# One more gate/up block by seven products, a second part made by an adding transfer, and later modulation sums: a hybrid decoder layer in float32

## The chip, the cores and the metric

The kernel runs on one core of one Trainium2 chip. The metric is the device time of one execution in microseconds (us), the median of three runs. Lower is better.

## What is computed

One decoder layer on 512 tokens of width 1024, all in float32:

```python
mods = (silu(c) @ w_ada + b_ada).reshape(9, D)          # shift, scale, gate for 3 sub-layers
h = rmsnorm(x, g_pre[0]) * (1 + sc1) + sh1
x = x + 0.5 * gt1 * rmsnorm((silu(h @ Wg) * (h @ Wu)) @ w_dn1, g_post[0])    # D_FF = 2816
h = rmsnorm(x, g_pre[1]) * (1 + sc2) + sh2
x = x + gt2 * rmsnorm(token_mixer(h), g_post[1])        # GLA heads and FoX attention, merged
h = rmsnorm(x, g_pre[2]) * (1 + sc3) + sh3
x = x + 0.5 * gt3 * rmsnorm((silu(h @ Wg2) * (h @ Wu2)) @ w_dn2, g_post[2])
```

## The kernel before

**Two parts.** TensorE multiplies float32 numbers as two float32r parts: a high part `hi` (the number rounded) and a low part `lo = x - hi`. A product is hi·hi + hi·lo + lo·hi, so three matmuls. For each weight tile `split` (L153 to L158) lets ScalarE (ACT) copy 128x1024 numbers of a raw tile into `whi` (L156) and VectorE (DVE) subtract to get `wlo` (L157). There are 4 raw tiles (`NRAW`) and 5 tiles each of `whi` and `wlo` (`NW`); a split needs the slot that was used five splits before, and gets it when TensorE is done with that product. `hilo` (L198 to L200) does the same for activations.

**The feed-forward layers.** The gate and up matrices are worked on in 11 blocks of 256 columns (`ffn`). Block 0 of the first layer is worked on during the start. A plain block is 96 matmuls of 512 columns (L381). Blocks 2, 3, 4, 6, 7, 8 and 9 (`SEVEN`) go through `seven`: gate and up of one block are taken as a 2x2 matrix of halves, and 7 products of 24 matmuls with 256 columns (L430) take the place of 8. What the left sides then need is 4 sums on VectorE (L414, L415, L418, L421, in place in the raw tiles) and 7 splits; the results need 5 additions out of PSUM (`plus`, L436), two products with SiLU (L457) and 4 `hilo`. The raw tiles are fetched in the order a11, a21, a22, a12; a12 is changed by L421 and then split last, as the left side of product 6 (`l4`). `u2` is the first `plus` of a block; product 3 writes the same PSUM bank and follows it.

**Order.** All loads are issued by SyncE (SP) from one queue. A scheduler sets the order on every engine; on each the order is then fixed, and an engine waits at an instruction until its inputs are there.

**Modulation.** `ada_acc` sums eight rows of blocks of `w_ada` times SiLU(c) on VectorE (L212, L214). What is left is a sum over the 128 partitions. For shifts and scales of the second and third sub-layer (`mod_cols`, 4 calls each) `mod_reduce` (L269) does it with 4 float32 matmuls of one column, which the profile shows as 8. The first four calls for the third sub-layer run during the attention; those for the second run at the end of the gate/up blocks and in `down`. For gates (`mod_gate`, 2 calls in each `down`) the sum is split in two parts, in a `wlo` tile, and two matmuls with a matrix of ones (L295, L296) add the partitions, before the matmuls of the group in which the call stands.

**Start.** `load_x` issues 8 loads of x (256 KB each) from SP, with four small loads between the first four.

## Time and profile before

| | |
|---|---|
| median of 3 runs | 1424.99 us (1424.88 to 1426.5) |
| the profiled execution's own time | 1423.47 us |
| its span, first to last instruction | 1421.7 us |
| TensorE matmul busy | 1361.7 us (96%) |
| VectorE, ScalarE, GpSimd busy | 913.4, 595.2, 206.3 us (64%, 42%, 15%) |
| mean granted TensorE clock | 0.992 of full speed |

The profile is of one execution. Busy time is the sum over an engine's instructions, whatever they waited for. Where TensorE is busy nearly all the time, other engines matter where it waits for them, and where they let it go on with fewer matmuls.

### The profile page before, as it was taken

The page shows a single profiled execution, that of the slowest core. Times are in us where ns is not written, and L with a number is a line of the kernel's source. Part 1 is how long each engine was busy: PE and PEld are TensorE (multiplying, and loading weights), DVE is VectorE, ACT ScalarE, POOL GpSimd, SP SyncE. Part 2 cuts the span into 40 slices and gives each one's busy share as a digit, 9 for nine tenths or more (in the row PEclk, how much of TensorE's full clock was granted, in tenths as well). Part 3 has the DMA queues.
Part 4 walks back from the last instruction along what each step waited for, and adds up shares of the span by engine and source line. Part 5 has one row for each costly group of instructions (what it writes and reads, how often), then busy time and mean ns, then how long its engine had stood idle before and what let it go on. Part 6 is the DMA issues. An engine that isn't in the chain of part 4 may idle for free.

```text
span 1421.7 us, 19490 instructions
## 1 busy us (share of the span) xinstructions
PE 1361.7 (96%) x7485; PEld 1146.0 (81%) x7485; DVE 913.4 (64%) x1410; ACT 595.2 (42%) x1026; POOL 206.3 (15%) x328
## 2 busy tenths in 40 slices
PE   4899999999999999999999999999999999999998
PEld 3699899878877777777888887788878989987886
DVE  6898688675266689762645546538577877867222
ACT  6444445213254476654633334423345444333121
POOL 5300000000060644340110202100060000000001
PEclk7999999999999999999999999999999999999999
DMA  9423234588336755322332222125631332346331
GB/s 323 141 70 118 76 104 133 177 281 265 93 107 189 229 159 166 90 75 84 94 105 74 74 75 60 60 74 154 217 119 53 111 119 75 104 134 202 125 118 59
DMA packets 164089, 180.84 MB, mean 127 GB/s; under 512 B 9226, under 2 KB 128118, under 8 KB 163996
## 3 DMA queue, kind: packets, MB, share of 16 engines
q1 hardware_dynamic: 163996, 179.60, 41.1%
q8 instruction: 59, 0.97, 0.3%
q14 instruction: 34, 0.28, 0.1%
HBM read 173.25 MB, written 6.32 MB: 126 GB/s over the span
## 4 chain that ended last, share of the span: by engine, by line
PE 71%; DVE 16%; DMA 4%; ACT 4%; issue 3%; POOL 1%; SPq 0%; DVEq 0%; POOLq 0%; ACTq 0%
PE mm L193 46%; PE mm L381 11%; PE mm L430 8%; DVE wlo L157 5%; DMA raw<-in_w_gu_dram 3%; PE aux L1074 1%; DVE u L200 1%; DMA raw<-in_w_dn_dram 1%; DVE t L436 1%; ACT whi L156 1%; PE mm L896 1%; PE aux L885 1%; ACT u L869 1%; PE aux L269 1%; DVE t L214 1%
## 5 line engine op out<-in xcount | busy, mean ns | idle before, releaser
L156 ACT CAST whi<-raw 128x1024 fp32r<-128x1024 f32 x262 | 273.4, 1050 | 521.5 <-PE mm L193 272.6
L157 DVE TENSOR_TENSOR wlo<-raw,whi 128x1024 fp32r<-128x1024 f32 x260 | 322.7, 1247 | 253.5 <-ACT whi L156 238.9
L193 PE MATMUL mm<-whi,u 128*128 128x512 f32 x1216 | 391.7, 398 | 1.5 <-DVE t L354 1.5
L193 PE MATMUL mm<-u,whi 128*128 128x512 f32 x896 | 288.8, 401 | 0.8 <-DVE u L1101 0.8
L430 PE MATMUL mm<-u,whi 128*128 128x256 f32 x1568 | 279.8, 281 | 7.7 <-DVE t L436 7.6
L193 PEld LDWEIGHTS mm<-whi,u 128*128 128x128 f32 x1216 | 228.2, 188 | 54.8 <-ACT u L199 1.7
L430 PEld LDWEIGHTS mm<-u,whi 128*128 128x128 f32 x1568 | 240.2, 188 | 10.9 <-DVE t L436 10.3
L193 PE MATMUL mm<-wlo,u 128*128 128x512 f32 x608 | 240.1, 395 | 0.0
L430 PE MATMUL mm<-u,wlo 128*128 128x256 f32 x784 | 219.2, 280 | 0.0
L193 PEld LDWEIGHTS mm<-u,whi 128*128 128x128 f32 x896 | 166.4, 188 | 39.0 <-DVE u L1101 1.2
L381 PE MATMUL mm<-u,whi 128*128 128x512 f32 (+1 forms) x576 | 168.5, 379 | 11.4 <-ACT u L199 10.2
L193 PE MATMUL mm<-u,wlo 128*128 128x512 f32 x448 | 177.9, 397 | 0.0
L430 PEld LDWEIGHTS mm<-u,wlo 128*128 128x128 f32 x784 | 147.4, 188 | 0.0
L193 PEld LDWEIGHTS mm<-wlo,u 128*128 128x128 f32 x608 | 114.3, 188 | 26.8
L381 PEld LDWEIGHTS mm<-u,whi 128*128 128x128 f32 x576 | 105.5, 191 | 35.4 <-ACT u L199 13.4
L381 PE MATMUL mm<-u,wlo 128*128 128x512 f32 (+1 forms) x288 | 105.5, 376 | 0.0
L193 PEld LDWEIGHTS mm<-u,wlo 128*128 128x128 f32 x448 | 84.4, 188 | 19.5
L308 POOL TENSOR_SCALAR sm<-ss 128x1 f32<-128x1 f32 x12 | 2.3, 190 | 642.2 <-ACT jk L315 642.2
L214 DVE SCALAR_TENSOR_TENSOR t<-raw,csil,t 128x512 f32<-128x512 f32 x98 | 74.4, 759 | 3.8 <-DMA raw<-in_w_ada_dram 1.1
L381 PEld LDWEIGHTS mm<-u,wlo 128*128 128x128 f32 x288 | 55.3, 192 | 10.4
L436 DVE TENSOR_TENSOR t<-mm,t 128x512 f32<-128x512 f32 x70 | 48.0, 685 | 12.1 <-PE mm L430 11.8
L842 POOL TENSOR_SCALAR u<-t,Ft 128x128 f32<-128x128 f32 (+1 forms) x64 | 42.1, 667 | 91.3 <-DMA t<-Fd 50.1
(199 smaller groups left out, 1378.2 us busy)
## 6 DMA issues: line engine op xcount, KB each, us to landing
raw<-in_w_gu_dram SPq DMA_DIRECT2D x88, 512.0 KB, 4.0
raw<-in_w_in_dram SPq DMA_DIRECT2D x64, 512.0 KB, 3.8
raw<-in_w_dn_dram SPq DMA_DIRECT2D x44, 512.0 KB, 4.9
raw<-in_w_ada_dram SPq DMA_DIRECT2D x64, 256.0 KB, 3.6
raw<-in_w_ada_dram SPq DMA_DIRECT2D x24, 512.0 KB, 4.0
u<-in_w_ada_dram SPq DMA_DIRECT2D x32, 256.0 KB, 6.5
raw<-in_w_in_dram SPq DMA_DIRECT2D x20, 256.0 KB, 2.9
u<-in_x_dram SPq DMA_DIRECT2D x16, 256.0 KB, 4.7
```

The costliest lines, as they stand in the source:

```text
L156: nc.scalar.copy(hi, raw)
L157: (eng or nc.vector).tensor_tensor(lo, raw, hi.bitcast(F32), ALU.subtract)
L193: nc.tensor.matmul(ps, a[i], b[j], start=first and n == 0, stop=last and n == 2)
L200: (eng or nc.vector).tensor_tensor(lo, src, hi.bitcast(F32), ALU.subtract)
L214: nc.vector.scalar_tensor_tensor(a, raw[:, j, :], csil[:, k:k + 1], a, ALU.mult, ALU.add)
L269: nc.tensor.matmul(ps[:, j:j + 1], a[:, j * P:(j + 1) * P], ones[:, 0:1], start=True, stop=True)
L381: nc.tensor.matmul(p_[:, ts], w_[k][i][:, cs], hs[k][e][:, ts], start=ks[0] == 0 and n == 0, stop=ks[-1] == KD - 1 and n == 3 * len(ks) - 1)
L430: nc.tensor.matmul(ps[:, j], left[i][:, k, j * P:(j + 1) * P], right(k, e), start=first and k + j + n == 0, stop=k == 3 and n == 2, skip_g ...
L436: nc.vector.tensor_tensor(o, ps, a, ALU.add)
L842: nc.gpsimd.tensor_scalar(s_at(s, i), fb[:, 0:n], -1.0, Ft[:, i, h:h + 1], ALU.mult, ALU.add)
L869: nc.scalar.activation(s_at(S[e], i), s_at(S[e], i), AF.Exp, bias=nmx[e][:, i:i + 1], accum_out=rs[e][:, i:i + 1])
L885: nc.tensor.transpose(tp[:, off:off + P], s_at(S[e], i)[:, j * P:(j + 1) * P], ident)
```

## The change

- **Blocks.** `SEVEN` is now 2 to 9, so block 5 goes through the seven products too, in both feed-forward layers: 8 blocks in a row instead of 3, a plain one and 4.
- **Second part by a transfer.** In every such block the split of product 6 is `split_added`: ScalarE writes the high part and then the negated number into the low part's tile (as float32r, thus minus the high part), and a DMA from GpSimd's queue adds the raw tile to it. The subtraction on VectorE goes away.
- **Modulation as rows.** `mod_cols` splits its sum in two parts at once; later two matmuls of 512 columns with the matrix of ones add the partitions, and four masked sums on VectorE (`tensor_tensor_reduce` with the identity) turn the row into columns. In `down` these run one group of weights later than before.
- **Gates.** The two matmuls of `mod_gate` run after the matmuls of the next group. The two parts stand in general tiles, no longer in a `wlo` slot.
- **Start.** Three of the eight loads of x are issued from ScalarE's queue.
- `seven` is rewritten as a class with the same steps.

```diff
-SEVEN = (2, 3, 4, 6, 7, 8, 9)
+SEVEN = tuple(range(2, 10))
...
-                i = nc.sync.dma_start(xt[t][h], src[t * P:(t + 1) * P, h * 512:(h + 1) * 512])
+                i = (nc.scalar if between and h else nc.sync).dma_start(
+                    xt[t][h], src[t * P:(t + 1) * P, h * 512:(h + 1) * 512])
...
-                if between:
+                if between and not h:
                     nc.sync.dma_start(*between.pop(0))
...
+    def split_added(raw, shape):
+
+        hi = sb.tile([P] + list(shape), F32R, tag="whi", bufs=NW, name=nm("whi"))
+        lo = sb.tile([P] + list(shape), F32R, tag="wlo", bufs=NW, name=nm("wlo"))
+        nc.scalar.copy(hi, raw)
+        nc.scalar.activation(lo, raw, AF.Copy, scale=-1.0)
+        nc.gpsimd.dma_start(lo.bitcast(F32), raw, accum_op=ALU.add)
+        return hi, lo
...
     def two_parts(a):
-        pair = sb.tile([P, 2, 512], F32R, tag="wlo", bufs=NW, name=nm("pair"))
-        hilo(pair[:, 0], pair[:, 1], a)
-        return pair[:, 0], pair[:, 1]
+        pair = unit(F32R), unit(F32R)
+        hilo(*pair, a)
+        return pair
...
         a = ada_acc(src)
 
+        hi, lo = two_parts(a)
+
         def rest():
-            mod_turn(shc, scc, i, ch, mod_reduce(a))
+
+            ps = aux()
+            nc.tensor.matmul(ps, ones_r, hi, start=True, stop=False)
+            nc.tensor.matmul(ps, ones_r, lo, start=False, stop=True)
+            own, col = tmp((P, P)), small(4)
+            for j in range(4):
+                nc.vector.tensor_tensor_reduce(own, ps[:, j * P:(j + 1) * P], ident, 1.0, 0.0,
+                                               ALU.mult, ALU.add, col[:, j:j + 1])
+            mod_turn(shc, scc, i, ch, col)
         return rest
...
-        ps = aux()
         hi, lo = two_parts(a)
-        nc.tensor.matmul(ps, ones_r, hi, start=True, stop=False)
-        nc.tensor.matmul(ps, ones_r, lo, start=False, stop=True)
-        nc.vector.scalar_tensor_tensor(gs, ps, factor, gs, ALU.mult, ALU.mult)
+
+        def rest():
+            ps = aux()
+            nc.tensor.matmul(ps, ones_r, hi, start=True, stop=False)
+            nc.tensor.matmul(ps, ones_r, lo, start=False, stop=True)
+            nc.vector.scalar_tensor_tensor(gs, ps, factor, gs, ALU.mult, ALU.mult)
+        return rest
...
+            if n == 1:
+                nc.vector.tensor_tensor(a21, a21, a22, ALU.add)
+                nc.vector.tensor_tensor(a11, a21, a11, ALU.subtract)
+            elif n == 3:
+                nc.vector.tensor_tensor(a21, a22, a11, ALU.subtract)
+            part = (a11, a11, a21, a21, a12, a22, a12)[n]
+            self.left.append((split_added if n in self.added else split)(part, (4, 256)))
+            if n == 4:
+                nc.vector.tensor_tensor(a12, a12, a11, ALU.subtract)
...
+        s = Seven(*gu_blocks(w_gu, jb), hs, rs, added=(6,))
+        for n in range(s.N):
+            s.prep(n)
+        for n in range(s.N):
+            s.run(n)
+        gates, ups = s.result()
...
-                if dh == 0 and k0 in (0, 4):
-                    gate(g, k0 // 4)
-                late = extra.pop(0)() if extra and dh == 0 and k0 > 4 and k0 % 4 == 0 else None
+                if dh == 0 and k0 % 4 == 0:
+                    rest = gate(g, k0 // 4) if k0 < 8 else extra.pop(0)() if extra else None
...
-                if late:
-                    late()
+                if dh == 0 and k0 % 4 == 2 and rest:
+                    rest()
```

The order on the engines moves at three places. **VectorE, second feed-forward layer, from block 8's last sums to block 9's first.** Before (L421 changes a12; then the splits of a22 and a12; L436 is `u2`; then the next block's split of a11 and its first sum L414, which reads a21 and a22):

```order
L421 TENSOR_TENSOR raw_11165<-raw_11165,raw_11159 128x1024
L157 TENSOR_TENSOR wlo_11192<-raw_11163,whi_11191 128x1024
L436 TENSOR_TENSOR t_2087_11252<-mm_11200,t_2086_11226 128x512
L157 TENSOR_TENSOR wlo_11196<-raw_11165,whi_11195 128x1024
L157 TENSOR_TENSOR wlo_11406<-raw_11397,whi_11405 128x1024
L414 TENSOR_TENSOR raw_11399<-raw_11399,raw_11401 128x1024
L436 TENSOR_TENSOR t_2088_11302<-mm_11200,t_2086_11226 128x512
L415 TENSOR_TENSOR raw_11397<-raw_11399,raw_11397 128x1024
```

Now, at the same place (L454, L167, L483, L447 and L448 are the old L421, L157, L436, L414 and L415):

```order
L454 TENSOR_TENSOR raw_11447<-raw_11447,raw_11441 128x1024
L167 TENSOR_TENSOR wlo_11474<-raw_11445,whi_11473 128x1024
L483 TENSOR_TENSOR t_2139_11535<-mm_11483,t_2138_11509 128x512
L167 TENSOR_TENSOR wlo_11689<-raw_11680,whi_11688 128x1024
L447 TENSOR_TENSOR raw_11682<-raw_11682,raw_11684 128x1024
L483 TENSOR_TENSOR t_2140_11585<-mm_11483,t_2138_11509 128x512
L448 TENSOR_TENSOR raw_11680<-raw_11682,raw_11680 128x1024
```

The split of a12 is gone from VectorE. The split of the next a11 stands ahead of L447 in every block now, and `u2` right behind the split of a22; before, both places differed from block to block.

**ScalarE at the same place.** Now (L471 is product 0's copy, L158 the high part of a12, L159 its negation, which GpSimd's queue follows with the adding transfer; then the next block's first high part):

```order
L166 CAST whi_11473<-raw_11445 128x1024
L209 CAST u_11423<-t_2116_11434 128x256
L209 CAST u_11425<-t_2116_11434 128x256
L471 COPY t_2138_11509<-mm_11482 128x512
L158 CAST whi_11477<-raw_11447 128x1024
L159 ACTIVATE wlo_11478<-raw_11447 128x1024
L166 CAST whi_11688<-raw_11680 128x1024
```

One pass of 128x1024 has come in between the high parts of a12 and of the next a11.

**TensorE, second gate of the last `down`.** Before:

```order
L193 MATMUL mm_11780<-wlo_11873,u_10053 128x512
L193 MATMUL mm_11780<-whi_11872,u_10054 128x512
L295 MATMUL aux_11898<-pair_11899,ones 128x512
L193 MATMUL mm_11777<-whi_11931,u_10289 128x512
L193 MATMUL mm_11777<-wlo_11932,u_10289 128x512
```

Now:

```order
L203 MATMUL mm_12064<-wlo_12214,u_10469 128x512
L203 MATMUL mm_12064<-whi_12213,u_10470 128x512
L317 MATMUL aux_12241<-u_12183,ones 128x512
L318 MATMUL aux_12241<-u_12184,ones 128x512
L203 MATMUL mm_12061<-whi_12247,u_10706 128x512
```

The gate's two matmuls stand two groups of 24 matmuls further down.

## Rows read from the trace of the kernel before

**Rows 1.** The page: busy time by engine, and the chain that ended last by engine.

```profile
PE 1361.7 (96%) x7485; PEld 1146.0 (81%) x7485; DVE 913.4 (64%) x1410; ACT 595.2 (42%) x1026; POOL 206.3 (15%) x328
...
PE 71%; DVE 16%; DMA 4%; ACT 4%; issue 3%; POOL 1%; SPq 0%; DVEq 0%; POOLq 0%; ACTq 0%
```

**Rows 2.** Windows: blocks 2-4, 5, 6-9 of both layers; busy us (instructions) by engine.

```profile
88.32:150.35 62.03, 60.26 (x506) 59.65 (x505) 52.41 (x63) 29.25 (x41) 0.00 (x0) 1.00 0.41 128
150.35:172.68 22.33, 22.33 (x98) 17.92 (x96) 12.17 (x15) 7.27 (x11) 0.00 (x0) 1.00 0.09 26
172.68:255.53 82.85, 80.46 (x674) 79.57 (x673) 69.57 (x82) 39.35 (x54) 0.00 (x0) 1.00 0.39 121
1099.24:1160.20 60.96, 60.12 (x506) 59.66 (x505) 51.47 (x61) 29.52 (x41) 0.00 (x0) 1.00 0.42 130
1160.20:1182.53 22.33, 22.33 (x97) 17.92 (x96) 12.16 (x15) 7.26 (x11) 0.00 (x0) 1.00 0.09 26
1182.53:1266.06 83.53, 80.81 (x674) 79.96 (x673) 69.63 (x82) 39.48 (x55) 0.00 (x0) 1.00 0.39 120
```

**Rows 3.** Timeline of VectorE, blocks 8 and 9, second layer: start, us, instruction, [idle before].

```profile
1214.35 1.22 DVE L414 TENSOR_TENSOR raw<-raw,raw 128x1024 f32<-128x1024 f32 x1 [3.18 <-DMA raw<-in_w_gu_dram]
...
1230.84 1.22 DVE L157 TENSOR_TENSOR wlo<-raw,whi 128x1024 fp32r<-128x1024 f32 x1
1231.97 0.68 DVE L436 TENSOR_TENSOR t<-mm,t 128x512 f32<-128x512 f32 x1
1232.58 2.35 DVE L157 TENSOR_TENSOR wlo<-raw,whi 128x1024 fp32r<-128x1024 f32 x2
1236.82 1.23 DVE L414 TENSOR_TENSOR raw<-raw,raw 128x1024 f32<-128x1024 f32 x1 [1.90 <-DMA raw<-in_w_gu_dram]
...
1251.87 2.35 DVE L157 TENSOR_TENSOR wlo<-raw,whi 128x1024 fp32r<-128x1024 f32 x2
```

**Rows 4.** Timeline of TensorE, same block: product 3's first matmuls; product 6's first low part.

```profile
1232.71 0.51 PE L430 MATMUL mm<-u,whi 128*128 128x256 f32 x2 [1.00 <-DVE t L436]
...
1241.90 0.28 PE L430 MATMUL mm<-u,wlo 128*128 128x256 f32 x1
```

**Rows 5.** Timeline of ScalarE, same block: the high part of a12.

```profile
1231.01 1.05 ACT L156 CAST whi<-raw 128x1024 fp32r<-128x1024 f32 x1 [1.74 <-DVE raw L421]
```

**Rows 6.** DMA issues of the whole run: count, KB each, median us from issue to landing.

```profile
raw<-in_w_gu_dram SPq DMA_DIRECT2D x88, 512.0 KB, 4.0
u<-in_w_ada_dram SPq DMA_DIRECT2D x32, 256.0 KB, 6.5
```

**Rows 7.** Timeline of TensorE in the first `down`: a modulation sum between weight matmuls.

```profile
308.16 0.39 PE L193 MATMUL mm<-whi,u 128*128 128x512 f32 x1
308.39 0.95 PE L269 MATMUL aux<-ones,t 128*128 128x1 f32 x8
309.20 0.48 PE L193 MATMUL mm<-whi,u 128*128 128x512 f32 x1
```

**Rows 8.** Groups of VectorE, shapes apart: count, busy us, mean ns of one, idle before.

```profile
L214 DVE SCALAR_TENSOR_TENSOR t<-raw,csil,t 128x512 f32<-128x512 f32 x98 | 74.4, 759 | 3.8 <-DMA raw<-in_w_ada_dram 1.1
...
L244 DVE SCALAR_TENSOR_TENSOR t<-u,csil,t 128x512 f32<-128x512 f32 x10 | 11.5, 1146 | 0.4
...
L860 DVE CUSTOM_DVE_ANT_0 u<-mm,u 128x128 f32<-128x128 f32 x16 | 4.5, 289 | 3.8 <-POOL u L844 3.2 <-PE mm L857 0.4
...
L200 DVE TENSOR_TENSOR pair<-t,pair 128x512 fp32r<-128x512 f32 x6 | 4.1, 689 | 3.3 <-ACT pair L199 3.3
```

**Rows 9.** Windows in the attention; columns as in rows 2.

```profile
500.00:520.00 20.00, 19.60 (x105) 14.33 (x103) 19.31 (x48) 14.91 (x36) 7.63 (x15) 1.00 0.43 122
540.00:560.00 20.00, 19.89 (x114) 15.72 (x114) 19.37 (x50) 12.81 (x31) 6.18 (x12) 1.00 0.56 149
```

**Rows 10.** Timeline of TensorE in the last `down`: the two gates.

```profile
1295.50 0.50 PE L295 MATMUL aux<-pair,ones 128*128 128x512 f32 x1 [0.88 <-ACT pair L199]
...
1308.37 0.49 PE L295 MATMUL aux<-pair,ones 128*128 128x512 f32 x1 [1.41 <-ACT pair L199]
```

**Rows 11.** Timeline of VectorE before the second of them: the next weights' low part.

```profile
1305.37 1.23 DVE L157 TENSOR_TENSOR wlo<-raw,whi 128x1024 fp32r<-128x1024 f32 x1 [0.84 <-ACT whi L156]
```

**Rows 12.** The chain in order of time, start of the program: start, us, what.

```profile
3.68 0.32 SPq L131
4.05 5.31 DMA u<-in_x_dram
```

More of the change, by code (lines that the diff above doesn't have):

```diff
@@ L400, in right_sides, with __init__, prep, run @@
         return [lambda k, e, s=s: s[k // 2][e][:, k % 2] for s in sums]
[L402 to L426 removed]
+    class Seven:
+        N = 7
+        def __init__(self, wa, wb, hs, rs, turned=False, added=()):
+            self.w, self.turned, self.added = (wa, wb), turned, added
+            b11, b21, b22 = [lambda k, e, k0=k0, ts=ts: hs[k0 + k][e][:, ts] for k0, ts in
+                             ((0, slice(0, 256)), (4, slice(0, 256)), (4, slice(256, 512)))]
+            t1, t2, t3, t4 = rs
+            self.right, self.left = (b11, t2, t1, t3, b21, t4, b22), []
+        def prep(self, n):
+            wa, wb = self.w
+            if n == 0:
+                wa.fetch(0, 4)
+                wb.fetch()
+                wa.fetch()
+                self.a = [wa.raw[0], wa.raw[4], wb.raw[0], wb.raw[4]]
+            a11, a12, a21, a22 = self.a
+            if n == 1:
[7 more added lines that the diff above has]
+                nc.vector.tensor_tensor(a12, a12, a11, ALU.subtract)
+        def run(self, n):
+            if n == 0:
+                self.x, self.y, self.z = [acc((P, 2, 256)) for _ in range(3)]
+            ps, first = (self.x, self.y, self.z, self.y, self.x, self.y, self.z)[n], n < 3
+            left, right = self.left[n], self.right[n]
@@ L427, in product @@
             for k in range(4):
                 for j in range(2):
-                    for n, (i, e) in enumerate(PARTS):
-                        nc.tensor.matmul(ps[:, j], left[i][:, k, j * P:(j + 1) * P], right(k, e),
-                                         start=first and k + j + n == 0, stop=k == 3 and n == 2,
-                                         skip_group_check=True)
-        def plus(ps, a, out=None):
+                    js = slice(j * P, (j + 1) * P)
+                    for m, (i, e) in enumerate(PARTS):
+                        w_, h_ = left[i][:, k], right(k, e)
+                        nc.tensor.matmul(ps[:, j], *((h_[:, js], w_) if self.turned else (w_[:, js], h_)),
+                                         start=first and k + j + m == 0, stop=k == 3 and m == 2,
+                                         skip_group_check=True)
@@ L435, in plus @@
+            if n == 0:
+                self.p1 = tmp((P, 2, 256))
+                nc.scalar.copy(self.p1, ps)
+            elif n == 1:
+                self.u2 = self.plus(ps, self.p1)
+            elif n == 3:
+                self.u3 = self.plus(ps, self.p1)
+                self.plus(self.z, self.u3, self.u3)
+            elif n == 6:
+                self.plus(self.y, self.p1, self.p1)
+                self.plus(ps, self.u2, self.u2)
+        def plus(self, ps, a, out=None):
             o = tmp((P, 2, 256)) if out is None else out
```

46 lines of the change are left out of this document (6 added, 40 removed).

## The prediction

> **What bounds the kernel now.** I read the page first: TensorE is busy 96% of the span, and the chain that ended last is TensorE for 71% and VectorE for 16% [rows 1]. So time is saved either by giving TensorE fewer columns or by taking away what it waits for. Then the windows over the blocks that the change touches. There the reader is to see three things [rows 2]. A plain block takes 22.33 us, with TensorE busy throughout. A block by seven products keeps TensorE busy for about 20.04 us (60.12 / 3). And the runs of such blocks take longer than that: 62.03 and 82.85 us in the first layer, 60.96 and 83.53 in the second, so TensorE waits 1.77, 2.39, 0.84 and 2.72 us in them, and the runs of four lose most. The eight blocks take 62.03 + 22.33 + 82.85 = 167.21 us in the first layer and 166.82 in the second.
>
> Next, what TensorE waits for. Product 3 of block 8 starts after a wait of 1.00 us for `u2` on VectorE [rows 4], and VectorE runs `u2` only at 1231.97, behind the split of a22 that began at 1230.84 [rows 3]. So VectorE's queue sets the pace at the end of a run. VectorE in turn has a cycle of its own, with the loads: L414 of block 8 starts at 1214.35 and that of block 9 at 1236.82, 22.47 us later. It consists of the work from L414 to the end of the split of a22 (at 1230.84 + 1.22 = 1232.06, so 17.71 us), which frees the raw tile, and of 4.76 us until the next a22 is there. In these 4.76 us VectorE has `u2` and two splits to do and then sits idle for 1.90 us.
>
> **Seven products eight times.** The change takes the split of a12 off VectorE: 1.22 us in each of 16 blocks. But at both places in rows 3 that split stands behind the split of a22, inside the wait for the load, which has idle time left (1.90 us, 3.18 in the cycle before). So its removal alone shortens nothing; only the idle time grows. What shortens the cycle is the place of the split of a11, which now always stands ahead of L447. Block 9 had this order already: from its L414 at 1236.82 to the end of its split of a22 (the first of the pair that begins at 1251.87, so about 1253.0) it took 16.2 us [rows 3]. With 4.76 us for the load that makes a cycle of 20.95 us.
>
> The adding transfer shares the DMA engines with the load of a22. No row of before shows such a transfer. Below, it costs nothing there, since the next load of a12, which now waits for it, used to stand in the same place. Above, it delays a22 by half of an ordinary transfer's 4.0 us [rows 6], 2.0. I take 0.2, near the lower end, since the load of a12 goes out of the way: cycle 21.15.
>
> The runs start with a lead, so the first blocks go at TensorE's pace. First layer: three blocks at 60.26 plus half of the old wait, 0.9, then five cycles of 21.15: 166.9, 0.3 less than before. Second layer, where the first three lost less and more lead is left: 60.12 + 0.2, two blocks at about 20.1 and 20.9, three cycles: 164.8, 2.0 less. Together **-2.3**. What 0.1 us more or less in the cycle does: 14 cycles follow on a first block, so 1.4 us.
>
> The adding transfer itself has to be ready for product 6. The high part of a12 ran from 1231.01 to 1232.06 [rows 5]; the second pass on ScalarE takes the same 1.05, so GpSimd can issue at 1233.1. Product 6 first reads its low part at 1241.90 [rows 4]. So 8.8 us are there for issue and transfer. Ordinary loads of the same size land after 4.0 us, and the slowest loads listed, in the burst at the start, after 6.5 [rows 6]. An adding transfer reads two operands and writes one; bounds are 4.0 and, three times that, 12.0. I take 6.5, so it is hidden. GpSimd's queue has nothing else there (0.00 us busy in all six windows [rows 2]). ScalarE pays 1.05 us per block and is busy for under half of these windows [rows 2]. SyncE's queue stands longer at the load of a12, but the load behind it, the next block's a11, waits for that block's last sum anyway.
>
> The Trainium skill has a rule against this part: its page "SBUF — State Buffer", section "Summary: rules for kernel authors", advises against hiding a transfer from GpSimd's queue under VectorE's work, since its descriptors cannot be written while VectorE holds the shared port. By that rule it would start late, in VectorE's idle time. No row of before has such a transfer. Rows do show the two engines in each other's way: VectorE's scaled sum took 1146 ns while GpSimd worked at the start, and 759 ns elsewhere [rows 8]. For the forecast I leave the 6.5 us; a late start is the first rival. On the other side, the page of the Trainium skill "DMA: Bandwidth & Descriptors", section "Anatomy of one DMA", fits 2.0 us plus bytes at 436 GB/s, an estimate of 3.2 us for 512 KB, by which the sum would stay as it is.
>
> **Modulation as rows.** One sum takes TensorE from 308.16 to 309.20, where two weight matmuls stand 0.23 us apart, so 0.81 us net; two matmuls of 512 columns take 2 x 0.23 = 0.47 [rows 7]. That is 0.34 us in each of 8 calls: -2.7. VectorE pays for it: 0.69 for the low part and four masked sums of 0.29 (the attention's reduction of the same shape), 1.85 us per call [rows 8]. In the attention VectorE is busy 19.31 and 19.37 of 20 us where TensorE is at 19.60 and 19.89 [rows 9]; there the cover is thin. Bounds for the four calls there: nothing, and 4 x 1.85 = 7.4 us. I take 1.4, nearer the lower end, since TensorE is not idle for more than 0.4 in those 20 us. Together **-1.3**.
>
> **Gates.** In the last `down` TensorE stops at both gates, for 0.88 and 1.41 us [rows 10], while the next weights' low part is ready at 1305.37 + 1.23 = 1306.60 [rows 11]. With the gates moved two groups down it can go on at 1306.6 in place of 1308.37: **-1.8**. Below: if the next weights are late too, nothing.
>
> **Start.** Three issues leave SyncE's queue; one takes 0.37 us there (from 3.68 to 4.05), and the chain runs over the loads of x for 5.31 us behind them [rows 12]. Between 0 and 3 x 0.37 = 1.1, as the loads share the same engines: **-0.6**.
>
> Sum: -2.3 - 1.3 - 1.8 - 0.6 = -6.0 us. The profiled execution took 1423.47 us, so 1417.5. The median of the runs is 1.5 above that execution, so **1419.0 us**, 0.4% less than 1424.99. Differences under 0.2% (2.85 us) cannot be told from none here.
>
> **Rivals.**
> 1. *The adding transfer comes late* (slower). Mechanism: it lands behind product 6's first low part, TensorE waits at that place in all 16 blocks. It decides from 8.8 us after ScalarE's second pass; each further us costs up to 16. At 10 us: 1.2 x 16 = 19, so 1438. For it: three streams in place of two, and rows 8. Against it: 4.0 and 6.5 [rows 6].
> 2. *The adding transfer slows the load of a22* by 0.7 us in place of 0.2. The cycle is then 21.65, 14 x 0.5 = 7.0 us more: 1426. For it: both begin within about 2 us of one another. Against it: the load of a12 no longer does.
> 3. *The attention pays for the masked sums* at 6 us in place of 1.4: 1423.6. For it, rows 9.
> 4. *VectorE was the bound by its sum of work, not by the cycle.* Then the split's removal lets TensorE go at its pace: 16 x 20.04 = 320.6 against 334.03, so -13.4 in place of -2.3: 1408. Against it: the idle 1.90 and 3.18 us ahead of L414 [rows 3].
>
> **Chances.** Forecast 0.55, rival 1 0.13, rival 2 0.17, rival 3 0.08, rival 4 0.07. Faster: most of the forecast (0.52), rival 4 and a little of rival 2: 0.61. Same: 0.03 of the forecast, half of rival 2 and most of rival 3: 0.17. Slower: 0.22. The range 1411 to 1431 takes in the forecast with its bounds (gates and start at nothing above, a cycle without the 0.2 and attention without the 1.4 below), rivals 2 and 3, and leaves out rivals 1 and 4.
>
> **What would show it.** Right: from one L447 to the next about 21 us in the later blocks, with over 2.5 us of idle time ahead of it that a load ends; product 6 without a wait; no wait at the gates; modulation sums of two matmuls that cost 0.47; eight blocks in 167 and 165 us. Wrong: TensorE waits for GpSimd's queue in product 6 (rival 1); the load of a22 takes over 5.3 us (rival 2); TensorE waits more in the attention (rival 3); blocks at 20.0 throughout (rival 4).

## The result, and the profile after

The changed kernel took **1461.34 us** (median of 4 runs, 1455.62 to 1461.75), the kernel before 1425.64 beside it (median of 4): ratio 1.0245, 95% interval 1.023 to 1.0261. It is 36 us slower; the forecast was 1419.0 with a range to 1431. The execution in the profile below took 1455.62 us for a span of 1453.9.

The page of the changed kernel, busy time by engine and the chain that ended last, answers to [rows 1]:

```profile
PE 1368.6 (94%) x7581; PEld 1152.6 (79%) x7581; DVE 928.7 (64%) x1494; ACT 620.2 (43%) x1062; POOL 221.2 (15%) x344
...
PE 63%; DVE 17%; DMA 10%; issue 4%; ACT 4%; POOL 2%; SPq 0%; DVEq 0%; ACTq 0%; POOLq 0%
```

No engine has much more to do than before. But in the chain the share of transfers has gone from 4% to 10%, and that of TensorE from 71% to 63%: the kernel now waits for loads.

Where the time went is read by taking the same matmul in both traces: the n-th weight matmul of `mm3`, of which both traces have 3288, and, in the columns at 406.70 and 1061.90, the same transposition behind the first `down` and behind `w_out`. How much later it starts than before (us):

| run | first `down` begins (278.66 before) | first `down` done (406.70) | attention done (652.40) | `w_out` done (1061.90) | in the last `down` (1296.31) | last matmul (1415.10) |
|---|---|---|---|---|---|---|
| changed | +2.73 | +9.98 | +31.44 | +31.51 | +32.50 | +32.10 |

So 2.7 us are lost by the end of the first layer's blocks, **7.3 in the first `down`, 21.4 between there and the end of the attention**, 2.4 in the second layer's blocks, and 1.8 comes back in the last `down`. (At the first matmul of the last `down`, 1288.38 before, it is +33.88; the column at 1296.31 stands behind the first gate, where 1.4 has come back already.) The two large losses lie where the modulation sums are made, not where the blocks are.

The profiled execution is the fastest of the four, 5.7 us under their median, so the pieces add up to 32.1 us and not to 36.

The windows over the eight blocks of each layer, with [rows 2] to compare (busy us of each engine, then the granted clock and the share of DMA):

```profile
87.64:258.59 170.95, 162.18 (x1346) 159.83 (x1345) 135.80 (x165) 85.23 (x118) 6.95 (x8) 1.00 0.46 129
1130.92:1299.95 169.03, 162.05 (x1346) 159.59 (x1345) 134.88 (x163) 85.67 (x118) 6.92 (x8) 1.00 0.47 130
```

Before it was 167.21 and 166.82 us; forecast were 166.9 and 164.8.

What happens in the first `down` is seen on VectorE's timeline, ahead of the first masked sum (start, us, instruction, idle time before it and what ended it). The kernel before, where L488 multiplies the first half of block 10 and L212 begins the next sum over `w_ada`:

```profile
272.50 0.69 DVE L488 TENSOR_TENSOR t<-t,mm 128x512 f32<-128x512 f32 x1 [7.70 <-PE mm L381]
...
274.60 0.49 DVE L212 TENSOR_SCALAR t<-raw,csil 128x512 f32<-128x512 f32 x1
```

and the changed one (L281 is the masked sum, L222 begins the next sum):

```profile
267.83 0.68 DVE L210 TENSOR_TENSOR u<-t,u 128x512 fp32r<-128x512 f32 x1
281.58 0.29 DVE L281 CUSTOM_DVE_ANT_0 t<-aux,ident 128x128 f32<-128x128 f32 x1 [13.07 <-PE aux L278]
...
285.17 0.48 DVE L222 TENSOR_SCALAR t<-raw,csil 128x512 f32<-128x512 f32 x1
```

VectorE stands for 13.07 us in front of the masked sum, which needs the row that TensorE makes only after block 10 (L278). Behind it in VectorE's queue, at 285.17, stands the next sum over `w_ada` (L222, then L224). Before, VectorE stood here too, for 7.70 us, but only for the first half of block 10, and the next sum began 4.1 us ahead of the first `down` (at 278.66); now it begins 3.8 us behind its start (281.38). The four raw tiles are full, and until VectorE has read them no load finds a free tile. The same stretch in the view of the transfers, 250 to 350 us in 40 slices of 2.5 us (busy tenths of the DMA engines, then GB/s):

```profile
DMA  9779886990000006889888889898505779837789
GB/s 242 225 229 304 302 236 219 350 340 24 0 0 0 0 2 219 247 308 373 294 276 284 268 286 277 294 324 240 196 13 148 236 244 325 302 93 248 229 285 339
```

and of the kernel before:

```profile
DMA  4845789400279889779879969989889977995899
GB/s 132 269 113 137 215 279 345 189 7 0 28 245 297 293 320 284 202 239 358 266 225 269 347 212 289 292 303 344 239 259 265 326 234 240 275 315 189 211 323 406
```

Before, the stream stops for two to three slices, now for six: 15 us without a load, from about 272 to 287 us, and TensorE runs out of weights:

```profile
291.19 1.65 PE L203 MATMUL mm<-whi,u 128*128 128x512 f32 x3 [4.05 <-ACT whi L166]
```

The stops cost more than their length. Windows of the first `down`, and from there to the end of the attention, before and changed; columns as in [rows 2]:

```profile
278.66:406.70 128.04, 127.78 (x562) 102.79 (x562) 69.53 (x96) 35.52 (x51) 5.74 (x16) 1.00 0.64 203
406.70:652.40 245.70, 236.10 (x1184) 183.58 (x1183) 175.65 (x401) 141.17 (x308) 100.29 (x176) 1.00 0.50 144
281.38:416.70 135.32, 129.70 (x544) 102.77 (x543) 78.06 (x137) 37.93 (x55) 6.23 (x16) 0.97 0.59 193
416.70:683.84 267.14, 243.78 (x1160) 184.82 (x1159) 184.73 (x437) 144.62 (x312) 100.27 (x176) 0.97 0.46 133
```

Of the 28.7 us that the two stretches lose, TensorE sits idle for 19.1; the other 9.6 are its own busy time, with fewer matmuls. The granted clock falls to half (1.2 instead of 2.4 GHz) around the stops: from 289.8 to 296.6 us, at the stop above,

```profile
289.80:296.60 6.80, 5.41 (x13) 4.15 (x14) 5.36 (x7) 2.61 (x3) 0.00 (x0) 0.50 0.90 299
```

and in the attention for 3.4, 10.2 and 3.4 us, from 463.9, 504.8 and 627.7 us on. Before, the mean granted clock from 44 to 1419 us is 1.00.

From 255 to 680 us VectorE waits for these rows seven times:

```profile
DVE t L281 <- PE aux L278: 33.1, 7, 13.1
```

(total, times, longest). Before, the same wait (L276 for L269) was a single one of 0.4 us in that stretch.

### The profile page after: what moved, and what is told of

It reads as the page before. It is cut to its first block, busy times and chain, and to the rows that moved or that the text cites. A ratio compares the mean times of both kernels' runs of the same rounds, so it can differ in the third digit from the quotient of the medians.

```text
span 1453.9 us, 19874 instructions
## 1 busy us (share of the span) xinstructions
PE 1368.6 (94%) x7581; PEld 1152.6 (79%) x7581; DVE 928.7 (64%) x1494; ACT 620.2 (43%) x1062; POOL 221.2 (15%) x344
## 4 chain that ended last, share of the span: by engine, by line
PE 63%; DVE 17%; DMA 10%; issue 4%; ACT 4%; POOL 2%; SPq 0%; DVEq 0%; ACTq 0%; POOLq 0%
PE mm L203 43%; PE mm L404 8%; PE mm L466 7%; DMA raw<-in_w_gu_dram 5%; DVE wlo L167 4%; ACT whi L166 2%; DMA raw<-in_w_in_dram 1%; PE aux L1118 1%; DVE t L483 1%; DMA u<-in_w_ada_dram 1%; DVE t L224 1%; DVE u L210 1%; DVE raw L447 1%; DVE u L917 1%; DMA raw<-in_w_ada_dram 1%
## 5 line engine op out<-in xcount | busy, mean ns | idle before, releaser
L166 ACT CAST whi<-raw 128x1024 fp32r<-128x1024 f32 x252 | 263.4, 1048 | 520.1 <-PE mm L203 258.5
L167 DVE TENSOR_TENSOR wlo<-raw,whi 128x1024 fp32r<-128x1024 f32 x250 | 311.2, 1247 | 253.0 <-ACT whi L166 250.9
L203 PE MATMUL mm<-whi,u 128*128 128x512 f32 x1216 | 394.1, 399 | 7.1 <-ACT whi L166 5.6
L466 PE MATMUL mm<-u,whi 128*128 128x256 f32 x1792 | 321.2, 282 | 15.7 <-DVE t L483 15.5
L203 PE MATMUL mm<-u,whi 128*128 128x512 f32 x896 | 290.0, 403 | 6.5 <-DVE sm L904 5.7
L466 PEld LDWEIGHTS mm<-u,whi 128*128 128x128 f32 x1792 | 274.5, 188 | 20.7 <-DVE t L483 15.3
L203 PEld LDWEIGHTS mm<-whi,u 128*128 128x128 f32 x1216 | 229.6, 189 | 62.8 <-ACT whi L166 6.9
L466 PE MATMUL mm<-u,wlo 128*128 128x256 f32 x896 | 251.2, 280 | 0.0
L203 PE MATMUL mm<-wlo,u 128*128 128x512 f32 x608 | 243.3, 400 | 0.7 <-DVE wlo L167 0.7
L203 PEld LDWEIGHTS mm<-u,whi 128*128 128x128 f32 x896 | 168.2, 191 | 46.1 <-DVE sm L904 6.2
L203 PE MATMUL mm<-u,wlo 128*128 128x512 f32 x448 | 179.2, 400 | 0.0
L466 PEld LDWEIGHTS mm<-u,wlo 128*128 128x128 f32 x896 | 168.8, 188 | 0.0
L404 PE MATMUL mm<-u,whi 128*128 128x512 f32 (+1 forms) x448 | 129.3, 377 | 9.7 <-ACT u L209 8.2
L203 PEld LDWEIGHTS mm<-wlo,u 128*128 128x128 f32 x608 | 115.1, 189 | 28.4 <-DVE wlo L167 2.1
L404 PEld LDWEIGHTS mm<-u,whi 128*128 128x128 f32 x448 | 82.5, 195 | 27.8 <-ACT u L209 13.0
L203 PEld LDWEIGHTS mm<-u,wlo 128*128 128x128 f32 x448 | 85.4, 191 | 20.2
L224 DVE SCALAR_TENSOR_TENSOR t<-raw,csil,t 128x512 f32<-128x512 f32 x98 | 76.1, 777 | 8.5 <-DMA raw<-in_w_ada_dram 6.4
L404 PE MATMUL mm<-u,wlo 128*128 128x512 f32 (+1 forms) x224 | 80.6, 372 | 0.0
L160 POOL DMA_DIRECT2D wlo<-raw x16 | 13.9, 867 | 376.2 <-ACT wlo L159 376.2
L209 ACT CAST u<-t 128x256 fp32r<-128x256 f32 (+1 forms) x106 | 46.4, 455 | 29.7 <-DVE t L533 15.4
L483 DVE TENSOR_TENSOR t<-mm,t 128x512 f32<-128x512 f32 x80 | 54.8, 685 | 4.0 <-PE mm L466 3.9
```

What stands on the lines that cost most here:

```text
L166: nc.scalar.copy(hi, raw)
L167: (eng or nc.vector).tensor_tensor(lo, raw, hi.bitcast(F32), ALU.subtract)
L203: nc.tensor.matmul(ps, a[i], b[j], start=first and n == 0, stop=last and n == 2)
L209: nc.scalar.copy(hi, src)
L224: nc.vector.scalar_tensor_tensor(a, raw[:, j, :], csil[:, k:k + 1], a, ALU.mult, ALU.add)
L404: nc.tensor.matmul(p_[:, ts], w_[k][i][:, cs], hs[k][e][:, ts], start=ks[0] == 0 and n == 0, stop=ks[-1] == KD - 1 and n == 3 * len(ks) - 1)
```

## The theories

**Theory A.** Each masked sum has a throw-away output, `own`, from the ring of four `tmp` buffers that the sums over `w_ada` come from too. With it in the ring, the order that is fixed when the kernel is built puts the masked sums ahead of the next modulation's sums; VectorE works in order, waits for TensorE, and the raw tiles stay full. **Rival B:** the masked sums cost their own time. **Rival C:** the adding transfers do it. For the sevens: **D**, the adding transfer slows the load of a22 beside it (rival 2 of the prediction); **E**, eight sevens without a plain block between them run at their buffer loop anyway; **G**, the extra pass on ScalarE.

The built order of VectorE shows what A speaks of. Before, in the attention (L212 and L214 are the next modulation's sum, L276 uses the columns of the one before):

```
L212 TENSOR_SCALAR t_772_4426<-raw_4427,csil 128x512
L214 SCALAR_TENSOR_TENSOR t_772_4426<-raw_4427,csil,t_772_4426 128x512
...
L214 SCALAR_TENSOR_TENSOR t_772_4426<-raw_4442,csil,t_772_4426 128x512 x2
L157 TENSOR_TENSOR wlo_4303<-raw_4300,whi_4302 128x1024
L276 SCALAR_TENSOR_TENSOR scc_3821<-aux_4272,cols 128x2
```

Now the next sum (L222) stands behind the masked sums (L281) of the one before:

```
L281 ISA t_764_4421,sm_4422<-aux_4418,ident 128x128
L281 ISA sm_4422 128x1
...
L297 TENSOR_TENSOR shc_3962<-sm_4422,cols 128x2
L222 TENSOR_SCALAR t_802_4576<-raw_4577,csil 128x512
```

## Experiments on the modulation sums

**1. The throw-away output into the sum's own buffer.**

```diff
-            own, col = tmp((P, P)), small(4)
+            col = small(4)
...
-                nc.vector.tensor_tensor_reduce(own, ps[:, j * P:(j + 1) * P], ident, 1.0, 0.0,
+                nc.vector.tensor_tensor_reduce(a[:, j * P:(j + 1) * P], ps[:, j * P:(j + 1) * P], ident, 1.0, 0.0,
```

> The changed kernel, but the throw-away output of the masked sums is written over the sum's own buffer and takes no buffer of the ring of four. Theory A (that buffer puts the masked sums ahead of the next modulation's sums in VectorE's queue, VectorE waits for TensorE, the raw buffers stay full and the weight stream stops): VectorE's waits for the row matmuls fall from 33 us to under 6 us, the stretch from the first down product to the end of attention loses some 28 us, time 1425 to 1432. Rival B (the masked sums cost time as such, whatever stands behind them): 1450 to 1461. Rival C (the adding transfers do the damage there): unchanged, 1458 to 1461.

Measured: 1437.9 us, ratio 1.0099 (1.0079 to 1.012). The wait for the rows is gone, from 33.1 us to

```profile
DVE t L281 <- PE aux L278: 1.9, 2, 1.0
```

and the first `down` costs nothing any more (+1.37 at its beginning, +1.11 at its end). The masked sums are all still there, so B cannot hold for `down`, nor C. But the attention still loses 8.0 us (+1.11 to +9.13), more than A said: the time is 6 us above its range.

**2. Columns again, all else as changed.**

```diff
-        hi, lo = two_parts(a)
-
         def rest():
...
+            mod_turn(shc, scc, i, ch, mod_reduce(a))
         return rest
```

> The changed kernel with the later modulation sums as columns again, all else as changed. Theories A and B: the 28 us of the first down product and attention come back, what is left is the sevens' loss of 3 to 6 us less gates and start: 1425 to 1431. Rival C (adding transfers): still 1450 to 1461.

Measured: 1433.01 us, ratio 1.0062 (1.0047 to 1.0077). First `down` +3.29 to +3.53, attention to +5.16: 1.6 us. So 27 to 28 us go with the rows, and C is out. What is left is somewhat more than foreseen.

**3. Rows alone, in the kernel before.** The edit is that of `mod_cols` and `two_parts` in the change.

> The kernel before with only the modulation rows and masked sums. Theories A and B: nearly the whole loss of the change, 1448 to 1458. Rival C (it needs the adding transfers): 1422 to 1427. The sum on record gave this part -1.3 us, 1423.6.

Measured: 1454.94 us, ratio 1.0214 (1.0199 to 1.0229). The part that the forecast had at -1.3 us costs 31 by itself: +0.44, +8.27, +30.95 at the first three places of the table.

**9. The ring buffer alone.** The kernel before, with its column sums; the four columns pass through one more buffer of the ring.

```diff
-            mod_turn(shc, scc, i, ch, mod_reduce(a))
+            ps = mod_reduce(a)
+            own = tmp((P, P))
+            nc.vector.tensor_copy(own[:, 0:4], ps)
+            mod_turn(shc, scc, i, ch, own)
```

> The kernel before with its column sums, and one buffer more of the ring of four per modulation sum: the four columns of the result are copied into it before they are used (one VectorE instruction of about 0.1 us, eight times). Theory A (the place in the ring orders VectorE's queue, not the masked sums' own time): the next modulation's sums stand behind the wait for TensorE, 1440 to 1455. Rival B (the masked sums' own time): eight tiny copies cost under 1 us, 1424 to 1427.

Measured: 1451.42 us, ratio 1.0177 (1.0159 to 1.0195): eight copies of 0.16 us cost **26 us**. VectorE's timeline at the first of them:

```profile
264.77 1.22 DVE L157 TENSOR_TENSOR wlo<-raw,whi 128x1024 fp32r<-128x1024 f32 x1
279.99 0.16 DVE L265 COPY t<-aux 128x4 f32<-128x4 f32 x1 [14.00 <-PE aux L272]
...
280.46 0.49 DVE L212 TENSOR_SCALAR t<-raw,csil 128x512 f32<-128x512 f32 x1
```

It is the picture of the changed kernel without a masked sum in it, the half clock included (a mean of 0.69 from 288 to 299 us). Theory A is shown: the place in the queue costs the time. In the first `down` the reason for that place is in the built programs: in the changed kernel and in run 9 the next sum gets the very buffer (the same address) that the extra tile has just had, so it cannot begin before that tile is read; in the kernel before and in run 1 it gets the one of block 10's first half, which is free sooner. In the attention it is another buffer. Which rule at build time makes this order out of one buffer more was not tried; that it does so is seen in the orders of the changed kernel and of runs 3 and 9, and that it doesn't without that buffer, in those of the kernel before and of run 1.

**8. Rows in the first `down` only**, with the output of run 1; columns in the attention.

```diff
+        if i == 2:
+            return lambda: mod_turn(shc, scc, i, ch, mod_reduce(a))
         hi, lo = two_parts(a)
```

> The changed kernel with the throw-away output in the sum's own buffer, rows only in the first down product and columns in attention. Theory F (what the run with the throw-away output moved still lost in attention, 8.0 us against 1.6 us with columns, is VectorE's extra work and its wait of 10 us for ScalarE's first parts of the sums): attention loses about 1.6 us, time 1430 to 1434. Rival (the 8 us there come from something that the down product leaves behind): 1436 to 1439.

Measured: 1431.12 us, ratio 1.0044 (1.0029 to 1.006). The attention loses 2.6 us (+1.40 to +4.01) where run 1 lost 8.0. So the rest of run 1 came from the rows in the attention. There VectorE does more (155.6 us busy in the 204 us from 446 to 650, against 148.4 in the 198 us from 448 to 646 in run 2), and it stands longer before the low parts, for ScalarE. Waits of VectorE from 440 us on to the end of the attention, run 1:

```profile
DVE u L210 <- ACT u L209: 10.0, 4, 4.4
```

In run 2 that wait is 3.5 us in two. Which of the two costs the time was not separated.

## Experiments on the blocks by seven

For these a cycle is cut in two: from one block's first addition (L447 in the changed kernel) to the end of the split of a22 on VectorE, which frees the raw tile of a22; and from there to the next block's first addition, which needs the next a22. Taken are all cycles under 26 us, from each kernel's profile; the means in us (time and ratio are of all executions of the run):

| kernel | cycles | whole | to a22's release | release to next addition | time, us | ratio to before |
|---|---|---|---|---|---|---|
| before | 6 | 21.84 | 17.15 | 4.69 | | |
| changed | 12 | 21.81 | 16.58 | 5.23 | 1461.34 | 1.0245 |
| 4: eight sevens, adding transfer | 12 | 22.17 | 16.61 | 5.57 | 1436.37 | 1.008 |
| 5: eight sevens, no transfer | 12 | 21.20 | 16.42 | 4.78 | 1425.61 | 1.0004 |
| 6: transfer, block 5 plain | 6 | 22.50 | 17.15 | 5.35 | 1427.66 | 1.002 |
| 10: half the bytes by transfer | 12 | 22.48 | 16.61 | 5.87 | 1442.01 | 1.0112 |
| 13: plain write beside | 12 | 22.75 | 16.52 | 6.23 | 1445.06 | 1.0151 |
| 14: extra ScalarE pass only | 12 | 21.41 | 16.59 | 4.83 | 1426.28 | 1.0002 |
| 15: transfer in two | 12 | 22.15 | 16.61 | 5.54 | 1434.89 | 1.0073 |

**4. Sevens and adding transfer alone, in the kernel before.** The edit is `SEVEN`, `split_added` and the class `Seven` of the change.

> The kernel before with block 5 by seven products and the last second part of every seven by the adding transfer, nothing else. If the two gate/up stretches lose here what they lose in the changed kernel (3.7 and 2.2 us): 1428 to 1433. The sum on record gave -2.3 us, 1422.7. By rival C 1450 or more.

Measured: 1436.37 us, ratio 1.008 (1.0061 to 1.0099), more than the two stretches of the changed kernel had said. The loss lies in the blocks: +6.92 at the end of the first layer's, and 6.2 more (from +9.67 to +15.91) by the beginning of the last `down`. The profiled execution, 1440.6 us, is the slowest of the four, so these pieces are somewhat too large.

**5. Block 5 by seven, without the transfer.**

```diff
-SEVEN = (2, 3, 4, 6, 7, 8, 9)
+SEVEN = tuple(range(2, 10))
```

> The kernel before with block 5 by seven products as well, no adding transfer. Theory D (the adding transfer makes the a22 load longer, and that load sits in the loop that sets a seven's period): with no such transfer each layer gains the plain block's 22.33 less 20.3 to 21.2 us, 1421 to 1424. Rival E (without a plain block between them the eight sevens run at their buffer loop, 21.5 us or more each, whether a transfer adds or not): 1428 to 1436, as with the adding transfer (1436.4).

Measured: 1425.61 us, ratio 1.0004 (0.9992 to 1.0017): no difference. It falls between the two expectations. E as stated is out, since eight sevens in a row run at 21.20 us a cycle. Of the gain that D gave, the profile shows -1.3 us at the end of the first layer's blocks; in the second layer 0.9 us are lost by the beginning of the last `down` (from -1.00 to -0.12). The ten executions of run 5 lie between 1421.35 and 1428.4 us, so pieces of about 1 us from one profile are no more than a hint. The adding transfer costs 11.8 us (+12.3 against +0.5, each to the kernel before beside it); 12 cycles, each 0.97 longer, make 11.6.

The reason is in the second half of the cycle. VectorE's timeline of run 4, the split of a22 and the next block's first addition (L433):

```profile
1202.17 1.22 DVE L166 TENSOR_TENSOR wlo<-raw,whi 128x1024 fp32r<-128x1024 f32 x1
...
1208.89 1.23 DVE L433 TENSOR_TENSOR raw<-raw,raw 128x1024 f32<-128x1024 f32 x1 [2.33 <-DMA raw<-in_w_gu_dram]
```

and of run 5 (the first of the pair is the split of a22, the second that of a12; L414 is the addition):

```profile
1168.23 2.35 DVE L157 TENSOR_TENSOR wlo<-raw,whi 128x1024 fp32r<-128x1024 f32 x2
...
1174.13 1.23 DVE L414 TENSOR_TENSOR raw<-raw,raw 128x1024 f32<-128x1024 f32 x1 [1.81 <-DMA raw<-in_w_gu_dram]
```

From the split's end to the addition it is 1208.89 - 1203.39 = 5.50 us in run 4 and 1174.13 - 1169.45 = 4.68 in run 5. Both times a load ends the wait. The split that the transfer replaces stands behind a22's release, so taking it away shortens nothing, and the load gets longer. What stands beside it has changed: SyncE issues the load of a22 0.06 us after the release in both runs, but the next load of a12 1.6 us after it in run 5 and 8.1 in run 4 (means), where that tile is free only when the transfer has landed. The transfer, issued 0.6 to 1.3 us after the release, takes the place beside the load of a22 that the load of a12 had.

**6. The adding transfer with block 5 plain.** The edit of run 4 with `SEVEN` as before.

> The kernel before with block 5 plain as it was and the adding transfer in the seven others. Theory D: 0.6 to 1 us lost per seven that follows a seven, 1430 to 1436. Rival E: no loss, 1422 to 1426.

Measured: 1427.66 us, ratio 1.002 (1.0009 to 1.0032), under the range of D though the cycles are longer by 0.66 (22.50 against 21.84). In this profile the first layer loses 2.85 us by the end of its blocks, the second 0.3 (from +3.84 to +4.10). That a plain block in the middle gives VectorE and the loads a lead of which the delay is paid would explain it; it was not tested. So the transfer and the eighth seven cost 2.6 and 0.5 us alone and 12.3 together.

**10. Half the bytes by the transfer.**

```diff
-        nc.scalar.activation(lo, raw, AF.Copy, scale=-1.0)
-        nc.gpsimd.dma_start(lo.bitcast(F32), raw, accum_op=ALU.add)
+        nc.scalar.activation(lo[:, 2:4], raw[:, 2:4], AF.Copy, scale=-1.0)
+        nc.gpsimd.dma_start(lo[:, 2:4].bitcast(F32), raw[:, 2:4], accum_op=ALU.add)
+        nc.vector.tensor_tensor(lo[:, 0:2], raw[:, 0:2], hi[:, 0:2].bitcast(F32), ALU.subtract)
```

> The run with eight sevens and the adding transfer, but the transfer takes half of the second part (256 KB) and VectorE the other half. Theory D (the transfer lengthens the a22 load that runs beside it): the stretch from the release of a22's buffer to the next block's first addition lies between 4.8 us (no transfer) and 5.6 us (512 KB), the time between 1425.6 and 1436.4: 1428 to 1433. Rival (a fixed price per transfer: its issue and ScalarE's extra pass): 1435 to 1438.

Measured: 1442.01 us, ratio 1.0112 (1.0098 to 1.0126): not between, but above. Half the bytes take nearly as long. The view of the transfers from 90 to 250 us, run 4 (KB each, median us to landing; then the queue's packets, MB and share):

```profile
q0 software_dynamic: 1008, 3.67, 11.6%
...
wlo<-raw POOLq DMA_DIRECT2D x7, 512.0 KB, 7.1
```

and run 10:

```profile
q0 software_dynamic: 1008, 1.84, 6.3%
...
wlo<-raw POOLq DMA_DIRECT2D x7, 256.0 KB, 6.3
```

The packets are as many (144 for each), the transfer is beside the load nearly as long. So the price does not go with the bytes, though the forecast had it so. One thing more differs: ScalarE's second pass is half as long, and the transfer is issued 0.55 us after a22's release (mean) where run 4 has 0.97. Whether the earlier start makes the dearer cycle was not tested.

**13. A plain write beside**, VectorE makes the low part.

```diff
-        nc.scalar.activation(lo, raw, AF.Copy, scale=-1.0)
-        nc.gpsimd.dma_start(lo.bitcast(F32), raw, accum_op=ALU.add)
+        nc.vector.tensor_tensor(lo, raw, hi.bitcast(F32), ALU.subtract)
+        away = dr.tile([P] + list(shape), F32, tag="away", bufs=2, name=nm("away"))
+        nc.gpsimd.dma_start(away, hi.bitcast(F32))
```

> Eight sevens, VectorE makes every second part (no adding transfer), and a plain, not adding transfer of 512 KB beside: the first part of the last piece is written out to DRAM from GpSimd's queue, after ScalarE has made it. Nothing waits for it. Theory D1 (any transfer beside the a22 load lengthens it): release of a22's buffer to next first addition 5.2 to 5.6 us, 1431 to 1437. Theory D2 (only the adding kind does, or its waits): 4.8 us as without, 1424 to 1427.

Measured: 1445.06 us, ratio 1.0151 (1.0119 to 1.0183), above the range. A write that nothing waits for costs 19 us: the second half of the cycle is 6.23 us. So a transfer need not be an adding one to lengthen the load of a22. How dear adding itself is, the run does not say: without it the load of a12 is back beside that of a22 (1.6 us after the release) and the write is a third stream, issued 0.1 us after the release on the mean.

**14. The extra pass on ScalarE without a transfer.**

```diff
-        nc.gpsimd.dma_start(lo.bitcast(F32), raw, accum_op=ALU.add)
+        nc.vector.tensor_tensor(lo, raw, hi.bitcast(F32), ALU.subtract)
```

> Eight sevens, no adding transfer, but ScalarE's second pass over the last piece is kept (VectorE then overwrites it). Theory G (a fixed price from ScalarE's extra pass): 1430 to 1437. Theories D1 and D2: 1424 to 1428.

Measured: 1426.28 us, ratio 1.0002 (0.999 to 1.0014). G is out: the pass is hidden.

**15. The transfer in two.**

```diff
-        nc.gpsimd.dma_start(lo.bitcast(F32), raw, accum_op=ALU.add)
+        for k in (0, 2):
+            nc.gpsimd.dma_start(lo[:, k:k + 2].bitcast(F32), raw[:, k:k + 2], accum_op=ALU.add)
```

> Eight sevens, the adding transfer as two of 256 KB each: the same bytes, twice the packets (288 for 144 per seven). If packets set what the a22 load loses (half the bytes in as many packets lost as much): the stretch grows from 5.6 to 6 us or more, 1442 to 1450. If the number of transfers or their bytes do not matter beside: 1435 to 1438.

Measured: 1434.89 us, ratio 1.0073 (1.0049 to 1.0096), as run 4. Twice the packets cost nothing more. So neither bytes nor packets scale the price, within 256 to 512 KB; what in the transfer does stays open. In all four runs the price is higher where the transfer is issued sooner (1.00, 0.97, 0.55 and 0.11 us after the release in runs 15, 4, 10 and 13), but the changed kernel, at 0.99, pays less than run 4, and no run moves the start alone.

## Experiments on gates and start, and the best version

**7. Gates later and x by two queues, nothing else.** The changed kernel with `SEVEN` of before, `added=()` and the columns of run 2.

> The changed kernel without its two other parts: sevens as before (block 5 plain, no adding), modulation sums as columns; what is left is the gate matmuls later and x by two queues. The sum on record gave -1.8 and -0.6 us: 1421 to 1423. Rival: the last modulation's later place costs what the gates give, 1424 to 1426.

Measured: 1423.12 us, ratio 0.9981 (0.9969 to 0.9994), -2.0 us where -2.4 was forecast. In its profile TensorE is 1.3 us ahead when block 2 begins, 0.4 behind when the last `down` begins (first matmul +0.36) and 2.0 ahead at the end.

**11 and 12. What gains, together.** Run 7 with the rows of run 8 in the first `down`; in run 11 also eight sevens without a transfer in the first layer alone, in run 12 not.

```diff
-        s = Seven(*gu_blocks(w_gu, jb), hs, rs, added=(6,))
+        s = Seven(*gu_blocks(w_gu, jb), hs, rs, added=())
...
-        by_seven=SEVEN, keep=(2, lambda tp, k: h3[tp, k // 2]), source=xe)
+        by_seven=(2, 3, 4, 6, 7, 8, 9), keep=(2, lambda tp, k: h3[tp, k // 2]), source=xe)
```

> What the runs so far say gains, together: gate matmuls later, x by two queues (-2.0 us together), rows in the first down product alone with the throw-away output in the sum's own buffer (-1.9), block 5 by seven without an adding transfer in the first layer alone (-1.3). Sum 1425.1 - 5.2 = 1420: 1418 to 1423. If the parts don't add up: 1423 to 1426.

Measured: 1420.32 us, ratio 0.9964 (0.9951 to 0.9976).

> The same with block 5 plain in both layers: 1.3 us more than with eight sevens in the first layer, 1420 to 1424; if block 5 by seven gave nothing there, the same time.

Measured: 1424.39 us, ratio 0.9994 (0.9984 to 1.0003): the rows gave nothing here, and the eighth seven 4.1 us, three times what run 5 had shown.

**16 and 17. The best again, beside the same without rows.** Run 17 is the kernel of run 11; run 16 has columns in the first `down`.

> Gates later, x by two queues, eight sevens without an adding transfer in the first layer alone, and modulation sums as columns everywhere. If the rows in the first down product give nothing (the run with block 5 plain and the rows took 1424.4, the one without the rows 1423.1): as fast as the best so far, 1419 to 1422. If they give 1.9 us, as the two earlier runs with the adding transfer had it: 1422 to 1424.

Measured: 1424.61 us, ratio 0.999 (0.998 to 1.0).

> The kernel of the best run once more, beside it on one chip: 1419 to 1422 if that time was no accident of its chip; 1423 or more if it was.

Measured: 1419.96 us, ratio 0.9963 (0.995 to 0.9976). So the version of runs 11 and 17 beats the kernel before by 0.37% and the changed one by 41 us, twice. The rows in the first `down` and the eighth seven in the first layer give that only together (4.6 us between runs 16 and 17, 4.1 between 12 and 11). In the first layer's blocks and `down` run 17 is 4.56 us ahead of before, run 16 2.96; why the one needs the other was not found.

## Why the prediction was wrong

**Modulation rows: the step that failed.** Forecast -1.3 us, measured +31 alone (run 3). The matmuls' own cost on TensorE was right: a row sum costs 0.46 us where 0.47 was forecast [rows 7]. Changed kernel, TensorE's timeline in the first `down`:

```profile
322.49 0.40 PE L203 MATMUL mm<-whi,u 128*128 128x512 f32 x1
322.73 0.40 PE L277 MATMUL aux<-u,ones 128*128 128x512 f32 x1
322.96 0.39 PE L278 MATMUL aux<-u,ones 128*128 128x512 f32 x1
323.19 0.40 PE L203 MATMUL mm<-whi,u 128*128 128x512 f32 x1
```

The mistake is in "VectorE pays for it: 0.69 for the low part and four masked sums of 0.29", with "Bounds for the four calls there: nothing, and 4 x 1.85 = 7.4 us". That prices the new instructions by their busy time and takes the upper bound from it too. An instruction that waits for TensorE costs what stands behind it: here the sums that free the raw tiles, behind them the loads, behind them TensorE. The first of these waits was 13.07 us alone, and after the stops TensorE ran at half its granted clock on top. Rival 3 named the attention as the place and VectorE as the engine, but priced it by the same busy time, and nothing was said of the first `down`, where 7.3 us went. What is left when the order is mended, 8.0 us in the attention against 1.6 with columns, is 6.4: there the bound of 7.4 did hold, and the value taken (1.4, "nearer the lower end, since TensorE is not idle") was wrong.

**Sevens: the second step.** Forecast -2.3, measured +12.3 alone (run 4). Two of its pieces held. The split taken off VectorE shortens nothing: run 5 has it, runs 4 and 15 don't, and the first half of the cycle is 16.42 us in the one and 16.61 in the others. And rival 1 was rightly set low: the transfer landed 6.4 us after its issue in the median, where 6.5 had been taken; page of the changed kernel:

```profile
wlo<-raw POOLq DMA_DIRECT2D x16, 512.0 KB, 6.4
```

and it was there 1.4 to 4.2 us before product 6 read it, in all 16 blocks. It was issued 0.3 us after ScalarE's second pass ended, never later. So the late start under VectorE's work, which the prediction drew from the Trainium skill's page "SBUF — State Buffer", section "Summary: rules for kernel authors", is not in this trace, though VectorE is busy for 79% of the first layer's window (135.80 of 170.95 us). That rule speaks of a VectorE in its 2x or 4x mode, a condition that the prediction left out; the trace does not tell the mode of an instruction. The estimate of 3.2 us by the Trainium skill's page "DMA: Bandwidth & Descriptors", section "Anatomy of one DMA", is half of what was measured.

What was mis-sized is the contention: "I take 0.2, near the lower end, since the load of a12 goes out of the way". Measured 0.45 in the changed kernel (5.23 against 4.78) and 0.79 in run 4; rival 2 had 0.7. The load of a12 did go out of the way, but the adding transfer took its place: it is issued 0.6 to 1.5 us after the release of a22 (1224.93 against 1223.69 in one block of the second layer) and takes 6.4, so it lies beside nearly the whole load of a22. Rival 2's mechanism is what happened, and its price per cycle was near.

The number to start from was wrong as well. Without the 0.2 in each of its 14 cycles the forecast stood at -5.1 (its sum gives only eight cycles the full 21.15, so the 14 do not fit it); run 5, without any contention, measured +0.5. Its cycle is 21.20 us where 20.95 had been worked out from [rows 3], and from block 2's first matmul to block 10's it takes 165.8 us in the first layer and 167.4 in the second (before 167.0 and 166.7), where 166.9 and 164.8 had been forecast with the 0.2. So the lead that the second layer was to have is not there; why was not found.

**Gates and start: right in the sum, partly by luck.** Forecast -1.8 and -0.6; run 7 gives -2.0 for both. The wait at the gates [rows 10] is gone. But the sum priced the second gate alone and put the first at nothing without a reason; in run 7 the first gives 1.1 us (from +0.36 to -0.76) and the second 1.2 (to -2.00). And the start gave 1.3 us by block 2, twice the forecast, of which nothing is left at the last `down`. In the changed kernel, behind the later place TensorE waits 0.75 us for weights (L203, at 1340.70), which the lower bound had foreseen.

The parts do not add up: +31, +12.3 and -2.0 make 41, and the change costs 36. That the sevens' delay is partly covered where VectorE and the loads are late already would explain it; it was not tested.

## What to carry to other kernels

An instruction that waits is priced by what stands behind it on its engine, in the built order, and by who waits for that; its own microseconds were the smallest part here (0.16 us a copy in run 9). Before a scratch output takes a buffer from a small ring, look where the ring's other users end up in the queue; write it over something that is dead. And a transfer put beside a load that sets the pace cost that load 0.45 to 1.45 us a cycle here, and what it freed elsewhere gained nothing: first ask which half of the loop the freed work stands in.

## What was not expected of the hardware

A transfer's price to a load beside it did not go with its bytes: 256 KB cost the a22 load 1.1 us (5.87 against 4.78), 512 KB 0.8 (5.57), and two of 256 KB 0.8 (5.54); halving the bytes took the transfer's own time only from 7.1 to 6.3 us. And a plain write of 512 KB to DRAM, landing after 5.4 us, cost 1.45 us a cycle (6.23), more than the adding one, though with the load of a12 beside it as well.
